# One encoder layer on one core: the values of two head groups by seven block products, the reversed rows gathered in steps, the kept weights prepared earlier

## The chip, the cores and the metric

The kernel runs on one core of a Trainium2 chip. The metric is the device time of one execution in microseconds (us). The engines are TensorE (PE in the profile, its weight loads PEld), VectorE (DVE), ScalarE (ACT), GpSimd (POOL) and SyncE (SP). SP and GpSimd also issue the DMA transfers. Each engine takes its instructions in the order in which the program lists them and waits at an instruction whose data aren't there.

## The reference, cut to what matters

One layer of an encoder, sequence 1024, width 1024, all in float32:

```
h = LN1(alpha*x + 0.5*SwiGLU_a(x))
h = LN2(alpha*h + HybridMixer(h))
h = LN3(alpha*h + 0.5*SwiGLU_b(h))

SwiGLU(x) = (silu(x @ w_gate) * (x @ w_up)) @ w_down        # inner width 2752
HybridMixer: p = h @ w_in + b_in  ->  q | k | v | u | gates
  attention: 12 heads in 3 groups of 4 with (window, dilation) = (128,1), (512,4), (2048,16)
  fourier:   real part of an FFT over positions and channels of u
  out = (g_attn * (attn @ w_proj_attn) + g_four * (four @ w_proj_fourier)) @ w_out
```

The change concerns v: `v = h @ w_in[:, v columns] + b_in[v columns]`, a product of 1024 x 1024 with 1024 x 1536. Its columns fall into three head groups of 512.

## The kernel before, in words

**Products.** Every float32 operand of a big product is split into a high and a low part (`split`, L324: ScalarE writes the high part at L330, VectorE the low one at L334), and each product runs as three matmuls: high by high, high by low, low by high (`TERMS`). One matmul is 128 x 128 by 128 x 512. The products of the feed-forward blocks and of the paired columns of the mixer (u, q with k, gates) are done in 2 x 2 blocks by seven block products in place of eight (`PROD`, L346: Winograd's form of Strassen's method). With rows in two halves and the inner dimension in two halves, the row operand has blocks a11, a12, a21, a22 and the sums s1 to s4 (`Operand.derive`, L385 and after), the weights have b11 to b22 and the sums t1 to t4. A pair of column blocks c takes seven jobs `J[c, 1..7]` of 12 matmuls.

**Order of the work.** The order is not written out by hand. Each piece is a node of a planner (`Flow`, L73): PE jobs in a fixed list, tasks for VectorE (V) and ScalarE (S, which stands for GpSimd's issues as well), loads (Q), and floating PE work (F). A node has a cost, what it depends on, a due job (`need`), a lead, and what it takes and gives back of three pools: 8 PSUM banks, `NPG` = 46 pages (128 x 1024) and `NS2` = 11 half pages. The planner steps through the jobs on a clock of its own and writes the program in the order that comes out. A load is put in the program when the due time less the lead is reached; a load that is far from due leaves 6 pages free. On the chip only the data's own waits hold; the planner's clock sets the order alone.

**The stages.** Feed-forward a: pairs of gate and up columns (a0 to a20) and a tail, its hidden blocks spilled to DRAM (`hsa...`), the weight sums for the down product made in DRAM (`tdat`: SP copies one block, L701, GpSimd adds another by an accumulating DMA, L704). Then the down product of block a (L741): block products 1, 6, 2, 5, 3, 7, 4, each in 11 steps of 12 matmuls, each step's operands loaded (L729, L730) with a lead of 44 us and split. Then norm 1 and its transposes (`tpY`), which give the row operand X2 (tiles `Ya...`) of the mixer. Then the values, the pairs u0, u1, q0 to q11 (with attention beside them) and s0 to s7, the two projections, the output product, norm 2, and feed-forward block b.

**The values before** (L1015 to L1051). Three groups of 512 columns, each 8 row tiles of 128 by one job of 24 matmuls: 8 inner blocks by three terms, into one bank. The order is group 0 rows 0 to 511, group 1 rows 0 to 511, group 0 rows 512 to 1023, group 1 rows 512 to 1023, group 2. Each group's weights are 4 pages, loaded by SP (L1029) and split. VectorE adds the bias (L1049) and GpSimd spills the result to `v_spill` (L1050), from which attention loads it later. `X2.derive` makes the blocks for the values and the sums s1 to s4 for the first u pair.

**The gather** (`reversed_rows`, L995). When pair a10's first product is done, GpSimd issues one after the other: the load of an index, an indirect load of 128 rows of `w_proj_fourier`, its store to `w_rev`, the second indirect load, its store. The two pages it takes are given back together.

**The kept weights** (`keep_parts`, L1400 and after). The two projections' weights (`wpa`, `wpf`, four quarters each) are loaded, the Fourier ones folded with the reversed rows (L1447, L1448), split, and the parts stored to DRAM (L1418), to be loaded again when the projections run. All eight are due at the job `early`, which is the first product of pair u0, with leads of 60 us (load) and 52 us (split).

Of the kernel before, what the change touches and what calls it, by code (L numbers as in the profile page):

```python
# [13 lines left out]
OP = mybir.AluOpType  # L14
AX = mybir.AxisListType

P = 128
S0 = 1024
D = 1024
KD = 8  # L20
# [52 lines left out]
class Flow:  # L73
# [21 lines left out]
    def V(self, *a, **kw):  # L95
        return self.task("V", *a, **kw)

    def S(self, *a, **kw):
        return self.task("S", *a, **kw)

    def Q(self, need, mb, fn, deps=(), lead=24.0, **kw):
        self.loads.append(Node("Q", mb, fn, deps, need, lead, **kw))
        return self.loads[-1]

    def F(self, us, fn, deps=(), banks=0, **kw):
        self.floats.append(Node("F", us, fn, deps, banks=banks, **kw))
        return self.floats[-1]
# [152 lines left out]
class Builder:  # L260
# [16 lines left out]
    def bank(self, name):  # L277
        return self.pp.tile([P, 512], F32, name=name, tag="ps", bufs=8)
# [6 lines left out]
def kernel(  # L285
# [38 lines left out]
    def split(name, get, put, deps=(), need=None, lead=14.0, w=1024, pages=2, gives=1):  # L324

        st = {}

        def hi():
            st["h"] = page(name + "h", F32R)
            nc.scalar.activation(st["h"][:, :w], get()[:, :w], AF.Copy)  # L330

        def lo():
            t = page(name + "l", F32R)
            nc.vector.tensor_sub(t[:, :w], get()[:, :w], st["h"][:, :w].bitcast(F32))  # L334
# [11 lines left out]
    PROD = {1: ("a11", "b11"), 2: ("a12", "b21"), 3: ("s4", "b22"), 4: ("a22", "t4"),  # L346
            5: ("s1", "t1"), 6: ("s2", "t2"), 7: ("s3", "t3")}
# [573 lines left out]
    X1, X2, X3 = Operand("X"), Operand("Y"), Operand("Z")  # L921
# [24 lines left out]
    COL_Q, COL_K, COL_V = 0, QW, 2 * QW  # L946
# [7 lines left out]
    w_rev = kb.dram([2 * P, D], "w_rev")  # L954
# [38 lines left out]
        return [S(0.0, lambda h=h: shears(h), [(n, 6.0 + 3.0 * h)]) for h in range(NH)]  # L993

    def reversed_rows():  # L995
        st = {}

        def gather():
            idx = kb.small([P, 2], "rev_idx", mybir.dt.int32)
            nc.gpsimd.dma_start(idx, c_rev)  # L1000
            for t in range(2):
                pg = page(f"rev{t}")
                nc.gpsimd.indirect_dma_start(out=pg, out_offset=None, in_=w_pf,
                                             in_offset=bass.IndirectOffsetOnAxis(ap=idx[:, t:t + 1], axis=0))
                nc.gpsimd.dma_start(w_rev[t * P:(t + 1) * P, :], pg)
        n = S(0.0, gather, [J[("a", 10), 1]], slack=20.0, pages=2)
        fl.later(n, 12.0, gives=2)
        return n

    shear_n = mixer_consts()  # L1010
# [1 line left out]


    v_d = kb.dram([S0, QW], "v_spill")
    VJ, v_stored = {}, {}  # L1015
# [3 lines left out]
    VJ[2, 7].back["p"] += 4  # L1019
    VW, vb = {}, {}  # L1020
    for g in range(3):
        def bias_row(g=g):
            vb[g] = half(f"vb{g}")
            nc.gpsimd.dma_start(vb[g], bcast_rows(b_in[COL_V + g * 512:COL_V + (g + 1) * 512], 512))
        qb = Q(VJ[g, 0], 0.25, bias_row, halves=1)
        for i in range(4):
            def load(i=i, g=g):
                VW[g, i] = t = page(f"wv{g}{i}")
                nc.sync.dma_start(t, in_values[g, i])  # L1029
            split(f"wv{g}{i}", lambda g=g, i=i: VW[g, i], lambda t, g=g, i=i: VW.__setitem__((g, i), t),  # L1030
                  [Q(VJ[g, 0], 0.5, load, pages=1)], VJ[g, 0], 20.0 if g else 14.0)
        VJ[g, 7].back["p"] += 8
        for m in range(8):
            st = {}

            def run(g=g, m=m, st=st):
                hf, mm = divmod(m, 4)
                ms = slice(mm * P, (mm + 1) * P)
                st["b"] = ps = bank(f"v{g}{m}")
                for k in range(KD):  # L1040
                    wv = [t.rearrange("p (k n) -> p k n", k=2)[:, k % 2, :] for t in VW[g, k // 2]]
                    for ti, (a, b) in enumerate(TERMS):
                        nc.tensor.matmul(ps, X2.cols(f"a{hf + 1}{k // 4 + 1}", a, k % 4)[:, ms], pick(wv, b),  # L1043
                                         start=(k == 0 and ti == 0), stop=(k == KD - 1 and ti == 2))
            VJ[g, m].fn = run

            def store(g=g, m=m, st=st):
                t = half(f"vs{g}{m}")
                nc.vector.tensor_add(t, st["b"], vb[g])  # L1049
                nc.gpsimd.dma_start(v_d[m * P:(m + 1) * P, g * 512:(g + 1) * 512], t)  # L1050
            v_stored[g, m] = V(0.69, store, [VJ[g, m], qb], frees=1, halves=1)  # L1051
            fl.later(v_stored[g, m], 3.0, hgives=1 + (m == 7))


    HEADS = [(g, h) for h in range(SLOTS) for g in range(3)]
# [7 lines left out]
    for g in range(3):  # L1063
        for m in range(8):
            VJ[g, m].after(*[X2.node[f"a{m // 4 + 1}{kh + 1}", i] for kh in range(2) for i in range(2)])
    for c in pairs:
        pair_weights(PC[c], in_pairs)
        for p in PROD:
# [470 lines left out]
    for gi in range(4):  # L1539
        st = {}  # L1540
# [6 lines left out]
        for i in range(2):  # L1547
# [24 lines left out]
            f = F(0.88, run, [q, (chan_ready, 10.0)], 1, gives=i)  # L1572
            n = S(0.42, hi, [f], pages=1 if s_ == 0 else 0, slack=2.0)
# [41 lines left out]
    for t in range(2):  # L1615
        st = {}
# [51 lines left out]
    f = F(1.7, mid_run, fold_n[0, 0] + fold_n[1, 0] + [pos_parts["n", 0]], 2)  # L1668
# [17 lines left out]
    n = V(0.6, mid_raw, [PJ[2]], pages=2, slack=20.0)  # L1686
# [12 lines left out]
    for c in range(8):  # L1699
        c2, cc = divmod(c, 2)  # L1700
        st = {}
# [20 lines left out]
    for c in range(8):  # L1722
        c2, cc = divmod(c, 2)
        st = {}
# [59 lines left out]
    for m in range(8):  # L1784
        st, sums = {}, kb.small([P, 4], "lw", bufs=9)
# [137 lines left out]
```

## Time and profile before

| | |
|---|---|
| median of three runs | 2103.39 us (2102.98 to 2103.85) |
| the profiled execution | 2102.25 us |
| its span, first to last instruction | 2100.5 us |
| mean granted TensorE clock | 0.998 |
| PE busy, weight loads busy | 2081.6 us (99%), 1732.6 us (82%) |
| VectorE, ScalarE, GpSimd busy | 1353.3, 766.6, 234.9 us |
| value matmuls (L1043) | 6.2% of the chain that ended last |

The profile is of one execution. Its page gives busy time by engine, the span in 40 slices, DMA queues, the chain of work that ended last, the costliest groups of instructions with what they waited for, and the DMA issues with their time to landing. The trace behind it can be asked for the instructions in order of time, for waits, and for busy time by stretches. In a row of a timeline the first number is the start in us from the span's start, the second the duration, and the bracket at the end the idle time of the engine before it and what ended that.

### The profile page before, as it was taken

Reading aid. Unit: us, or ns where it says so; the run is one execution under the profiler, and the core shown is the slowest. Engines: PE = TensorE matmul, PEld = TensorE weight load, DVE = VectorE, ACT = ScalarE, POOL = GpSimd, SP = SyncE. Lnnn points to the kernel's source line nnn. Section 1 sums busy time; section 2 is a strip of 40 time slices with the busy share of each in tenths; the row PEclk is TensorE's granted clock in tenths of the full one; section 3 lists DMA queues with packets and bytes.
Section 4 is the critical chain, followed back from the end, with each engine's and each line's share of the span. In section 5 each row is a group of like instructions: output and inputs, shape, how many; then the busy total and the mean of one; then the engine's idle time right before and its main releaser. Section 6 shows DMA issues by size and latency. Waiting matters only on the chain.

```text
span 2100.5 us, 25488 instructions
## 1 busy us (share of the span) xinstructions
PE 2081.6 (99%) x9619; PEld 1732.6 (82%) x9619; DVE 1353.3 (64%) x1856; ACT 766.6 (36%) x1175; POOL 234.9 (11%) x411
## 2 busy tenths in 40 slices
PE   9999999999999999999999999999999999999998
PEld 7888888888888888888888888888788888888886
DVE  6766666673575278556666654767766666675566
ACT  4322222362353132444445433315332222245332
POOL 0121211000001120022132101000001001010000
PEclk9999999999999999999999999999999999999999
DMA  4357876596643275567876439432223223267753
GB/s 160 126 181 218 256 191 192 162 342 224 207 174 142 84 277 147 173 166 201 216 200 168 167 126 370 156 136 101 86 91 116 95 90 136 82 232 273 235 180 105
DMA packets 141658, 366.66 MB, mean 175 GB/s; under 512 B 18066, under 2 KB 40338, under 8 KB 141152
## 3 DMA queue, kind: packets, MB, share of 16 engines
q1 hardware_dynamic: 104608, 244.36, 33.6%
q0 software_dynamic: 36928, 120.68, 19.7%
q8 instruction: 75, 1.23, 0.2%
q14 instruction: 47, 0.39, 0.1%
HBM read 277.18 MB, written 137.06 MB: 197 GB/s over the span
## 4 chain that ended last, share of the span: by engine, by line
PE 86%; issue 2%; DVE 1%; ACT 0%; DMA 0%; POOL 0%; DVEq 0%; POOLq 0%; ACTq 0%
PE Bb L422 7%; PE v L1043 6%; PE Ab L422 5%; PE Db L422 5%; PE Bq L422 5%; PE Ba L422 4%; PE Dq L422 3%; PE Aq L422 3%; PE Bs L422 3%; PE Zb L741 3%; PE Xb L741 3%; PE Za L741 3%; PE Xa L741 3%; PE Da L422 2%; PE wo L1798 2%; PE Aa L422 2%
## 5 line engine op out<-in xcount | busy, mean ns | idle before, releaser
L1049 DVE TENSOR_TENSOR vs<-v,vb 128x512 f32<-128x512 f32 x24 | 16.5, 691 | 61.0 <-PE v L1043 60.7
L1293 ACT ACTIVATE p<-p,stat 128x192 f32<-128x192 f32 (+2 forms) x96 | 42.3, 442 | 24.6 <-DVE stat L1288 23.9
L533 POOL DMA_DIRECT2D hsba<-r2b x19 | 10.3, 543 | 329.8 <-DVE r2b L603 329.8
L1280 DVE SCALAR_TENSOR_TENSOR p<-sc,bias 128x512 f32<-128x512 f32 (+1 forms) x40 | 24.8, 620 | 27.9 <-PE sc L1266 21.6
L533 POOL DMA_DIRECT2D hsaa<-r2a x19 | 11.0, 580 | 282.0 <-DVE r2a L603 282.0
L1325 PEld LDWEIGHTS pv<-pT,v 128*128 128x128 f32 (+1 forms) x320 | 37.1, 189 | 5.2
L1325 PE MATMUL pv<-pT,v 128*128 128x128 f32 (+1 forms) x320 | 40.6, 289 | 0.0
L501 ACT ACTIVATE r1a<-Aa 128x512 f32<-128x512 f32 x19 | 11.3, 597 | 73.0 <-PE Aa L422 73.0
L509 DVE TENSOR_TENSOR r3q<-Bq,r1q 128x512 f32<-128x512 f32 x12 | 8.3, 691 | 42.8 <-PE Bq L422 42.8
L587 ACT ACTIVATE sga<-Aa 128x512 f32<-128x512 f32 x19 | 11.4, 599 | 64.7 <-PE Aa L422 64.7
L587 ACT ACTIVATE sgb<-Ab 128x512 f32<-128x512 f32 x19 | 11.4, 598 | 63.8 <-PE Ab L422 63.8
L509 DVE TENSOR_TENSOR r3b<-Bb,r1b 128x512 f32<-128x512 f32 x19 | 13.1, 692 | 32.7 <-PE Bb L422 32.7
L590 DVE TENSOR_TENSOR r3b<-Db,r3b 128x512 f32<-128x512 f32 x19 | 13.1, 691 | 32.5 <-PE Db L422 32.5
L1266 PE MATMUL sc<-oq,oq 128*128 128x192 f32 (+2 forms) x192 | 33.8, 322 | 0.0
L590 DVE TENSOR_TENSOR r3a<-Da,r3a 128x512 f32<-128x512 f32 x19 | 13.1, 691 | 29.3 <-PE Da L422 29.1
L1266 PEld LDWEIGHTS sc<-oq,oq 128*128 128x128 f32 x192 | 29.9, 190 | 2.0
L1467 POOL DMA_DIRECT2D comb_t<-stat x48 | 29.2, 616 | 10.9 <-DMA stat<-stat 10.9
L501 ACT ACTIVATE r1b<-Ab 128x512 f32<-128x512 f32 x19 | 11.4, 598 | 47.7 <-PE Ab L422 47.7
L939 POOL DMA_DIRECT2D y_spill<-y x8 | 4.3, 537 | 215.3 <-DVE y L907 215.3
L493 DVE TENSOR_TENSOR usa<-ua,usa 128x512 fp32r<-128x512 f32 x19 | 13.1, 692 | 21.0 <-ACT usa L489 20.9
L422 PE MATMUL Da<-Xs40h,usa 128*128 128x512 f32 x76 | 26.5, 389 | 0.0
L422 PE MATMUL Da<-Xs41h,usa 128*128 128x512 f32 x76 | 26.5, 389 | 0.0
(7408 smaller groups left out, 7252.8 us busy)
## 6 DMA issues: line engine op xcount, KB each, us to landing
qa<-hsas SPq DMA_DIRECT2D x44, 256.0 KB, 3.8
qa<-tdat SPq DMA_DIRECT2D x44, 256.0 KB, 4.2
qb<-hsbs SPq DMA_DIRECT2D x44, 256.0 KB, 4.4
ga<-in_ffn_gu_dram SPq DMA_DIRECT2D x21, 512.0 KB, 4.2
ua<-in_ffn_gu_dram SPq DMA_DIRECT2D x21, 512.0 KB, 6.2
gb<-in_ffn_gu_dram SPq DMA_DIRECT2D x21, 512.0 KB, 3.5
ub<-in_ffn_gu_dram SPq DMA_DIRECT2D x21, 512.0 KB, 3.7
qa<-hsaa SPq DMA_DIRECT2D x33, 256.0 KB, 5.3
```

Of the source, the lines that this page charges most:

```text
L422: nc.tensor.matmul(out, pick(w, a)[:, k * P:(k + 1) * P], self.cols(xn, b, k), start=first and k == 0 and ti == 0, stop=last and k == 3 an ...
L501: nc.scalar.activation(H[c, "t1"], B[c, "A"], AF.Copy)
L587: nc.scalar.activation(H[c, "s0"], B.pop((c, "A")), AF.Silu)
L590: nc.vector.tensor_sub(H[c, "t3"], B[c, "D"], H[c, "t3"])
L741: nc.tensor.matmul(B[tag, set_, m], pick(q, a)[:, m * P:(m + 1) * P], pick(q, b)[:, R], start=first and j == 0 and ti == 0, stop=j == PAIR ...
L1043: nc.tensor.matmul(ps, X2.cols(f"a{hf + 1}{k // 4 + 1}", a, k % 4)[:, ms], pick(wv, b), start=(k == 0 and ti == 0), stop=(k == KD - 1 and ...
L1266: nc.tensor.matmul(sv[:, i, :], qk[0][:, qt * P:(qt + 1) * P], qk[1][:, k0:k0 + w], start=True, stop=True, skip_group_check=True)
L1280: stt(p3(), sv, scale, bv, op0=OP.mult, op1=OP.add)
L1293: nc.scalar.activation(p3()[:, i, :], p3()[:, i, :], AF.Exp, bias=stats[h][:, k, 0:1], scale=1.0, accum_out=stats[h][:, k, 1:2])
L1325: nc.tensor.matmul(out_of(tiles.index(qt)), env["v"][kc, rows], pt[r0:r0 + rows, sl * P:(sl + 1) * P], start=qt not in seen, stop=last, sk ...
L1467: nc.gpsimd.dma_start(dst, bass.AP(tensor=sd.tensor, offset=sd.offset + 48 * p0 + 2 * col, ap=ap))
L1798: nc.tensor.matmul(bk[i], pick(merged[k], a)[:, ms], pick(wo[k], b)[:, i * 512:(i + 1) * 512], start=(k == 4 * gi and ti == 0), stop=(k == ...
```

## The change: what it does

Three things, in one diff.

**Values of groups 0 and 1.** These two groups now form the two column blocks of one 2 x 2 block product: rows in two halves, inner dimension in two halves, columns group 0 and group 1. Seven block products (`VORDER`) replace eight; each is four jobs (one for each of four row tiles) of 12 matmuls into the banks A (products 1, 2), B (6, 7, 4) and D (5, 3). Group 2 keeps its jobs, now called `VJ["g", m]`: its rows 0 to 511 come first, then products 1 and 2, then its rows 512 to 1023, then products 6, 7, 5, 4, 3. The weights' sums t1 to t4 are made in DRAM ahead of time, as the down product's are: an SP copy due at the first product of pairs a2 to a5 and an accumulating GpSimd DMA due at the fifth product of pairs a3 to a6, 1 MB each. VectorE makes the result blocks from the banks (`value_sums`) with bias rows of its own. `X2.derive` is due at the value products in place of the first u pair.

**The gather** is issued in steps: the index when pair a6's first product is done, then gather, store, gather, store, each 16 us (on the planner's clock) after the one before, one page at a time, given back 6 us after its store.

**The kept weights** are due at step 8 of product 2 of the first down product (`J["a", "d", 2, 8]`).

```diff
-        def gather():
-            idx = kb.small([P, 2], "rev_idx", mybir.dt.int32)
-            nc.gpsimd.dma_start(idx, c_rev)
-            for t in range(2):
-                pg = page(f"rev{t}")
-                nc.gpsimd.indirect_dma_start(out=pg, ...
-                nc.gpsimd.dma_start(w_rev[t * P:(t + 1) * P, :], pg)
-        n = S(0.0, gather, [J[("a", 10), 1]], slack=20.0, pages=2)
-        fl.later(n, 12.0, gives=2)
+        st, n = {}, S(0.0, lambda: nc.gpsimd.dma_start(idx, c_rev), [J[("a", 6), 1]], slack=20.0)
+        for t in range(2):
...
+            n = S(0.0, gather, [(n, 16.0)], slack=20.0, pages=1)
+            n = S(0.0, store, [(n, 16.0)], slack=20.0)
+            fl.later(n, 6.0, gives=1)
...
-    for g, hf in ((0, 0), (1, 0), (0, 1), (1, 1), (2, 0), (2, 1)):
-        for m in range(4 * hf, 4 * hf + 4):
-            VJ[g, m] = job(24 * MM, None, 1)
+    VORDER = ((1, "A", True), (2, "A", False), (6, "B", True), (7, "B", False), (5, "D", True), (4, "B", False),
+              (3, "D", False))
+    def value_job(p, bk, new):
+        def product(m):
...
+                xn, wn = PROD[p]
+                for k in range(4):
+                    w = [t.rearrange("p (k n) -> p k n", k=2)[:, k % 2, :] for t in VW[wn, k // 2]]
+                    for ti, (a, b) in enumerate(TERMS):
+                        nc.tensor.matmul(B["v", bk, m], X2.cols(xn, a, k)[:, m * P:(m + 1) * P], pick(w, b), ...
+        for m in range(4):
+            VJ[p, m] = job(12 * MM, product(m), int(new), gives=4 if m == 3 else 0)
+    for m in range(4):
+        VJ["g", m] = job(24 * MM, None, 1)
+    for p, bk, new in VORDER:
+        value_job(p, bk, new)
+        if p == 2:
+            for m in range(4, 8):
+                VJ["g", m] = job(24 * MM, None, 1)
+    VJ["g", 7].back["p"] += 12
+    for i, (to, x0, x1) in enumerate((("t1", "b11", "b12"), ("t3", "b12", "b22"), ("t2", "t1", "b22"),
+                                      ("t4", "t2", "b21"))):
+        def copy(to=to, x0=x0):
+            nc.sync.dma_start(vt[to], vblk[x0] if x0 in vblk else vt[x0])
+        def add(to=to, x1=x1):
+            nc.gpsimd.dma_start(vt[to], vblk[x1], accum_op=OP.add, max_dma_last_dim=4096)
+        n = Q(J[("a", 2 + i), 1], 1.0, copy, [vtn[x0]] if x0 in vtn else [], lead=0.0)
+        vtn[to] = Q(J[("a", 3 + i), 5], 1.0, add, [n], lead=0.0)
...
+        n1 = V(0.69, t1, [VJ[1, m], q1], VJ[2, m], pages=new_page)
+        v_stored[0, m] = V(0.69, c11, [VJ[2, m], n1], frees=1, halves=1)
+        n2 = V(0.69, t2, [n1, VJ[6, m]], VJ[7, m], halves=1)
+        n3 = V(0.69, t3, [n2, VJ[7, m]], VJ[4, m], pages=new_page)
+        n4 = v_stored[1, m + 4] = V(0.69, c22, [n3, VJ[5, m]], VJ[3, m], halves=1, gives=m % 2)
+        n5 = V(0.4, z21, [n3, qs])
+        v_stored[0, m + 4] = V(0.69, c21, [n5, VJ[4, m]], frees=1, halves=1, gives=m % 2)
+        v_stored[1, m] = V(0.69, c12, [n4, VJ[3, m]], frees=1)
...
-    X2.derive({"a11": VJ[0, 0], "a12": VJ[0, 0], "a21": VJ[0, 4], "a22": VJ[0, 4]},
-              {p: J[PC["u", 0], p] for p in PROD}, 30.0)
+    X2.derive({"a11": VJ["g", 0], "a12": VJ["g", 0], "a21": VJ["g", 4], "a22": VJ["g", 4]},
+              {p: VJ[p, 0] for p in PROD}, 30.0)
...
-    early = J[PC["u", 0], 1]
+    early = J["a", "d", 2, 8]
```

More of the change, by code (lines that the diff above doesn't have):

```diff
@@ L995, in reversed_rows, with gather, store @@
     def reversed_rows():
-        st = {}
-        def gather():
-            idx = kb.small([P, 2], "rev_idx", mybir.dt.int32)
-            nc.gpsimd.dma_start(idx, c_rev)
-            for t in range(2):
-                pg = page(f"rev{t}")
-                nc.gpsimd.indirect_dma_start(out=pg, out_offset=None, in_=w_pf,
-                                             in_offset=bass.IndirectOffsetOnAxis(ap=idx[:, t:t + 1], axis=0))
-                nc.gpsimd.dma_start(w_rev[t * P:(t + 1) * P, :], pg)
-        n = S(0.0, gather, [J[("a", 10), 1]], slack=20.0, pages=2)
-        fl.later(n, 12.0, gives=2)
+        idx = kb.small([P, 2], "rev_idx", mybir.dt.int32)
+        st, n = {}, S(0.0, lambda: nc.gpsimd.dma_start(idx, c_rev), [J[("a", 6), 1]], slack=20.0)
+        for t in range(2):
+            def gather(t=t):
+                st[t] = page(f"rev{t}")
+                nc.gpsimd.indirect_dma_start(out=st[t], out_offset=None, in_=w_pf,
+                                             in_offset=bass.IndirectOffsetOnAxis(ap=idx[:, t:t + 1], axis=0))
+            def store(t=t):
+                nc.gpsimd.dma_start(w_rev[t * P:(t + 1) * P, :], st[t])
+            n = S(0.0, gather, [(n, 16.0)], slack=20.0, pages=1)
+            n = S(0.0, store, [(n, 16.0)], slack=20.0)
+            fl.later(n, 6.0, gives=1)
         return n
@@ L1014 @@
     v_d = kb.dram([S0, QW], "v_spill")
-    VJ, v_stored = {}, {}
-    for g, hf in ((0, 0), (1, 0), (0, 1), (1, 1), (2, 0), (2, 1)):
-        for m in range(4 * hf, 4 * hf + 4):
-            VJ[g, m] = job(24 * MM, None, 1)
[L1019 to L1041, printed above, removed]
-                    for ti, (a, b) in enumerate(TERMS):
[L1043 to L1052, printed above, removed]
@@ new lines, with run @@
+    VJ, v_stored, VW, vb, VT = {}, {}, {}, {}, {}
+    VORDER = ((1, "A", True), (2, "A", False), (6, "B", True), (7, "B", False), (5, "D", True), (4, "B", False),
+              (3, "D", False))
+    def value_job(p, bk, new):
+        def product(m):
+            def run():
+                if new:
+                    B["v", bk, m] = bank(f"v{bk}{m}")
+                xn, wn = PROD[p]
+                for k in range(4):
+                    w = [t.rearrange("p (k n) -> p k n", k=2)[:, k % 2, :] for t in VW[wn, k // 2]]
+                    for ti, (a, b) in enumerate(TERMS):
+                        nc.tensor.matmul(B["v", bk, m], X2.cols(xn, a, k)[:, m * P:(m + 1) * P], pick(w, b),
+                                         start=new and k == 0 and ti == 0, stop=k == 3 and ti == 2,
+                                         skip_group_check=True)
+            return run
+        for m in range(4):
+            VJ[p, m] = job(12 * MM, product(m), int(new), gives=4 if m == 3 else 0)
@@ new lines, in value_row, with run, value_part, load @@
+    def value_row(key, g, need):
+        def run():
+            vb[key] = half(f"vb{key}")
+            nc.gpsimd.dma_start(vb[key], bcast_rows(b_in[COL_V + g * 512:COL_V + (g + 1) * 512], 512))
+        return Q(need, 0.25, run, halves=1)
+    def value_part(name, i, src, deps, need, lead):
+        def load():
+            VW[name, i] = t = page(f"wv{name}{i}")
+            nc.sync.dma_start(t, src)
+        split(f"wv{name}{i}", lambda: VW[name, i], lambda t: VW.__setitem__((name, i), t),
+              [Q(need, 0.5, load, deps, lead + 10.0, pages=1)], need, lead)
@@ new lines, in store_values, with run, store @@
+    def store_values(t, m, g):
+        nc.gpsimd.dma_start(v_d[m * P:(m + 1) * P, g * 512:(g + 1) * 512], t)
+    q2 = value_row(2, 2, VJ["g", 0])
+    for i in range(4):
+        value_part("g2", i, in_values[2, i], (), VJ["g", 0], 14.0)
+    for p, bk, new in VORDER:
+        n = PROD[p][1]
+        for i in range(2):
+            value_part(n, i, (vblk if n in vblk else vt)[n][i], [vtn[n]] if n in vtn else (), VJ[p, 0], 14.0)
+    for m in range(8):
+        st = {}
+        def run(m=m, st=st):
+            hf, mm = divmod(m, 4)
+            st["b"] = ps = bank(f"v{m}")
+            for k in range(KD):
+                wv = [t.rearrange("p (k n) -> p k n", k=2)[:, k % 2, :] for t in VW["g2", k // 2]]
+                for ti, (a, b) in enumerate(TERMS):
+                    nc.tensor.matmul(ps, X2.cols(f"a{hf + 1}{k // 4 + 1}", a, k % 4)[:, mm * P:(mm + 1) * P], pick(wv, b),
+                                     start=(k == 0 and ti == 0), stop=(k == KD - 1 and ti == 2))
+        VJ["g", m].fn = run
+        def store(m=m, st=st):
+            t = half(f"vs{m}")
+            nc.vector.tensor_add(t, st["b"], vb[2])
+            store_values(t, m, 2)
+        v_stored[2, m] = V(0.69, store, [VJ["g", m], q2], frees=1, halves=1)
+        fl.later(v_stored[2, m], 3.0, hgives=1 + (m == 7))
@@ new lines, with both_rows, value_sums, page_half @@
+    q0, q1 = value_row(0, 0, VJ[1, 0]), value_row(1, 1, VJ[1, 0])
+    def both_rows():
+        vb["s"] = half("vbs")
+        nc.vector.tensor_add(vb["s"], vb[0], vb[1])
+    qs = V(0.4, both_rows, [q0, q1], VJ[6, 0], halves=1)
+    def value_sums(m):
+        def page_half(key):
+            k, i = (key, m // 2), m % 2
+            if k not in VT:
+                VT[k] = page(f"v{key}{m // 2}")
+            return VT[k][:, i * 512:(i + 1) * 512]
+        def t1():
+            nc.vector.tensor_sub(page_half("t1"), B["v", "A", m], vb[1])
+        def c11():
+            t = half(f"v00{m}")
+            nc.vector.tensor_add(t, B.pop(("v", "A", m)), vb[0])
+            store_values(t, m, 0)
+        def t2():
+            VT["t2", m] = t = half(f"vt2{m}")
+            nc.vector.tensor_add(t, B["v", "B", m], VT["t1", m // 2][:, (m % 2) * 512:(m % 2) * 512 + 512])
+        def t3():
+            nc.vector.tensor_add(page_half("t3"), B["v", "B", m], page_half("t1"))
+        def c22():
+            t = half(f"v11{m}")
+            nc.vector.tensor_sub(t, B["v", "D", m], page_half("t3"))
+            store_values(t, m + 4, 1)
+        def z21():
+            nc.vector.tensor_add(page_half("t1"), page_half("t1"), vb["s"])
+        def c21():
+            t = half(f"v01{m}")
+            nc.vector.tensor_add(t, B.pop(("v", "B", m)), page_half("t1"))
+            store_values(t, m + 4, 0)
+        def c12():
+            t = VT.pop(("t2", m))
+            nc.vector.tensor_sub(t, B.pop(("v", "D", m)), t)
+            store_values(t, m, 1)
+        new_page = 1 if m % 2 == 0 else 0
+        n1 = V(0.69, t1, [VJ[1, m], q1], VJ[2, m], pages=new_page)
[6 more added lines that the diff above has]
+        v_stored[1, m] = V(0.69, c12, [n4, VJ[3, m]], frees=1)
+        for key in ((0, m), (1, m + 4), (0, m + 4), (1, m)):
+            fl.later(v_stored[key], 3.0, hgives=1)
@@ L1055 @@
+    for m in range(4):
+        value_sums(m)
+    S(0.0, lambda: None, [v_stored[0, m] for m in range(4)] + [qs], hgives=2)
+    S(0.0, lambda: None, [v_stored[0, m] for m in range(4, 8)], hgives=1)
     HEADS = [(g, h) for h in range(SLOTS) for g in range(3)]
```

10 lines of the change are left out of this document (7 added, 3 removed).

## The prediction

> **What bounds the kernel now.** I read the page's head, then the chain that ended last through the stage that changes, then busy time by stretches.
>
> ```profile
> span 2100.5 us, 25488 instructions
> PE 2081.6 (99%) x9619; PEld 1732.6 (82%) x9619; DVE 1353.3 (64%) x1856; ACT 766.6 (36%) x1175; POOL 234.9 (11%) x411
> PE 86%; issue 2%; DVE 1%; ACT 0%; DMA 0%; POOL 0%; DVEq 0%; POOLq 0%; ACTq 0%
> ```
>
> ```profile
> 644.34 5.44 PE v L1043 x24
> 649.78 0.93 PE tpY L373 x8
> 650.71 5.51 PE v L1043 x24
> 656.22 2.62 PE tpY L373 x24
> 658.84 119.72 PE v L1043 x528
> 778.56 2.72 PE Au L422 x12
> ```
>
> TensorE (PE) is busy through the span and the chain is PE. Busy time alone could flatter it, since matmuls overlap; the second fence settles it. The value product (L1043) runs as 576 matmuls, 528 of them in one unbroken piece of 119.72 us, which is 0.2267 us each; 24 take 5.44 us, the same pace; and the next product (Au) starts where the last value matmul ends. So here a matmul fewer is 0.2267 us less, as long as nothing else ends last.
>
> The other engines and the DMA, by stretches (columns: length, busy us of PE, PEld, VectorE, ScalarE, GpSimd with counts, granted clock, DMA share, GB/s):
>
> ```profile
> 440.00:460.00 20.00, 20.00 (x90) 16.56 (x89) 17.49 (x16) 13.81 (x13) 0.00 (x0) 1.00 1.04 387
> 460.00:520.00 60.00, 60.00 (x266) 49.69 (x265) 22.83 (x25) 21.66 (x23) 0.00 (x0) 1.00 0.72 245
> 520.00:580.00 60.00, 60.00 (x266) 49.69 (x265) 35.05 (x41) 22.10 (x21) 0.00 (x0) 1.00 0.60 193
> 680.00:720.00 40.00, 40.00 (x178) 33.12 (x177) 6.08 (x9) 4.25 (x4) 4.58 (x9) 1.00 0.15 53
> 720.00:780.00 60.00, 60.00 (x267) 49.69 (x266) 43.52 (x49) 15.97 (x16) 14.64 (x28) 1.00 0.76 276
> ```
>
> The first three lie in the first down product, which ends at 644, the last two in the value stage. PE is full and its clock whole in all. VectorE idles in 680 to 720, and DMA has room almost everywhere; 387 GB/s is the most that a row here shows.
>
> **Part 1: the values of two groups by seven block products.** Removed: 16 products of 24 matmuls, 384. Added: 7 block products x 4 row tiles x 12 matmuls, 336, of the same shape and pace. Group 2 keeps its 192. So 48 matmuls go: 48 x 0.2267 = **-10.88 us** on PE, if the new order never makes it wait. What could make it wait:
>
> ```profile
> L1049 DVE TENSOR_TENSOR vs<-v,vb 128x512 f32<-128x512 f32 x24 | 16.5, 691 | 61.0 <-PE v L1043 60.7
> 668.37 1.22 DVE L334 TENSOR_TENSOR Ya221l<-Ya,Ya221h 128x1024 fp32r<-128x1024 f32 x1
> 709.01 1.06 ACT L330 ACTIVATE wv20h<-wv 128x1024 fp32r<-128x1024 f32 x1 [45.12 <-PE v L1043]
> 760.85 0.68 DVE L1447 TENSOR_TENSOR wpf3s<-wpf 128x512 f32<-128x512 f32 x1
> wv<-in_in_values_dram SPq DMA_DIRECT2D x12, 512.0 KB, 5.1
> ```
>
> VectorE: 24 additions of 0.691 us become 8 for group 2, 32 for the block sums and one of bias rows, 17 more, +11.7 us; weight splits go from 12 to 18, 6 x 1.22 = +7.3 us; the four kept-weight preparations that leave (part 3) take away 8 x 1.22 + 8 x 0.68 = 15.2 us. Net +3.8 us, in a stage whose two rows above hold 49.6 of 100 us: covered on average. The operand's s1 to s4 are now wanted by product 6, not by the u pair. The last row split they wait for ends at 669.6 (668.37 + 1.22). Product 6 stands after 8 products of group 2 and 8 block products: 644.34 + 3.55 of transposes + 12 x 5.44 = 713.2. That leaves 43.6 us for six sums and the first two splits, 8 x 1.22 = 9.8 us. Within the block products each PSUM sum has 3 jobs of 2.72 us between the product it reads and the next one on that bank, against 0.69. Costed at nothing; if that cover went, one sum is 0.69 us.
>
> Pages are the tight resource. NPG is 46; row 709.01 shows the price of waiting for them: ScalarE stood 45.12 us until a value product released pages. After the change the four a21 pages and the eight of group 2 come back only when g7 ends, just as product 6 begins. By my count from the code about 44 are then held (32 of the row operand and its sums, 8 of group 2, 4 of weights or value sums, 2 of LN constants, less what was given back). Product 7's two weight pages may start loading only then: landing 5.1, ScalarE 1.06, VectorE 2 x 1.22, in sum 8.6 us against the 10.88 us of product 6: covered, by 2.3 us. If product 6's own weights had to wait so, nothing would cover it: 8.6 us. Bounds 0 and +8.6; a gain is excluded, since PE already runs there without a gap. I take **+0.7**, near the covered end, since only a late DMA or a busy VectorE uses up the 2.3 us.
>
> **Part 2: the weight sums in DRAM.** Four copies on SP's queue and four accumulating stores on GpSimd's, 1 MB each, beside the first pairs of the first feed-forward block. The DMA has room: 162 GB/s in 100 to 140 below. The chain is what matters: the copy for t4 waits on SP until the add for t2 has landed, and the weight loads of pair a7 stand behind it.
>
> ```profile
> 100.00:140.00 40.00, 40.00 (x176) 32.31 (x175) 28.21 (x43) 10.73 (x14) 9.80 (x20) 1.00 0.48 162
> 113.65 0.33 SPq L452 DMA_DIRECT2D ga<-in_ffn_gu_dram  x1
> 118.24 0.33 SPq L452 DMA_DIRECT2D ua<-in_ffn_gu_dram  x1
> 122.82 0.51 POOL L982 DMA_DIRECT2D lines_d<-line  x1 [0.33 <-DVE line L981]
> 137.62 1.05 ACT L330 ACTIVATE ga7h<-ga 128x1024 fp32r<-128x1024 f32 x1
> 147.48 0.69 DVE L590 TENSOR_TENSOR r3a<-Da,r3a 128x512 f32<-128x512 f32 x1 [2.03 <-PE Da L422]
> tdat<-in_ffn_down_dram POOLq DMA_DIRECT2D x8, 1024.0 KB, 11.7
> ga<-in_ffn_gu_dram SPq DMA_DIRECT2D x21, 512.0 KB, 4.2
> ```
>
> The add for t2 stands on GpSimd behind the three lines_d stores, by its due time (fifth product of pair a5), so it goes at about 123.4 and lands 11.7 us later, at 135.1. The add for t4 in turn holds GpSimd until its copy lands; behind it stand spills of the hidden blocks, which nobody reads before the down product: no cost. Only then can SP go on; a7's load, until now at 113.65, lands at 139.3, 1.7 us after ScalarE's split ga7h took place at 137.62. ScalarE and VectorE work in order, so what stands behind that split moves with it, up to r3a, which PE needs; row 147.48 shows 2.03 us of idle VectorE there as cover. Bounds 0 and +4 (both loads and a whole split on PE's path); I take **+0.5**. The Trainium skill (DMA: Bandwidth & Descriptors, section Anatomy of one DMA) fits a GpSimd DMA as 2.0 us plus the bytes at 436 GB/s, an estimate of 4.4 us for 1 MB; the trace's 11.7 us for an accumulating one disagrees, and by the page this term would be zero and the time 2092.8.
>
> **Part 3: the gather in steps.** Now GpSimd issues index, gather, store, gather, store in one go and waits inside:
>
> ```profile
> 220.06 1.92 POOL L1003 DMA_INDIRECT rev<-in_w_proj_fourier_dram,rev_idx  x1 [4.13 <-ACT t12a11h L330]
> 234.09 0.56 POOL L1005 DMA_DIRECT2D w_rev<-rev  x1 [6.70 <-DMA rev<-in_w_proj_fourier_dram,rev_idx]
> 237.28 1.22 DVE L334 TENSOR_TENSOR ga12l<-ga,ga12h 128x1024 fp32r<-128x1024 f32 x1 [2.07 <-DMA w_rev<-rev]
> 242.25 0.39 PE L422 MATMUL Da<-Xs11h,t12a11l 128*128 128x512 f32 x1
> 242.90 0.50 PE L422 MATMUL Ba<-Xa220h,t34a11h 128*128 128x512 f32 x1 [0.26 <-DVE r3a L509]
> ```
>
> The second store is issued at 234.09; the split that gets its page waits 2.07 us, and PE starts two matmuls 0.65 us apart instead of 0.23: 0.42 us lost. With 16 us between gather and store, and between store and next gather, that wait goes; next late there is nothing but PE. **-0.42** (0 to -0.65).
>
> **Part 4: the kept weights beside the down product.** Their due time moves from product Au at 778.56 to step 8 of down product 2, three steps of 2.72 us before product 5 begins:
>
> ```profile
> 460.82 0.32 SPq L729 DMA_DIRECT2D qa<-hsas  x1
> 520.63 59.84 PE Za L741 x264
> ```
>
> That is 512.5, and with a lead of 60 us the first load comes at about 452. So 8 loads and 16 stores of 0.52 MB, 12.6 MB, and VectorE's 15.2 us move into 452 to 520. VectorE has 22.83 of 60 us there, and GpSimd, whose queue takes the stores, has nothing at all. DMA: 387 - 245 = 142 GB/s free gives 8.5 MB in the 60 us; the other 4.1 MB run on into 520 to 580, which has room for 11.6. On SP the eight loads stand among the loads of the down steps. Their cover is prefetch: the step loaded at 460.82 is multiplied from 520.63 on, 59.8 us later. Costed at **0**; without that cover it is the second rival. The gathers come four pairs earlier and are done long before 452. In the value stage the same work leaves the stretch 720 to 780, so its load falls.
>
> **The sum.** -10.88 + 0.7 + 0.5 - 0.42 + 0 = -10.10 us. The profiled execution took 2102.25 us (span 2100.5), so 2092.15 there; the median of the runs shown, 2103.39, stands 1.14 above it. Forecast: **2093.3 us**. A measurement of this kernel tells about 0.2% from no change, 4.2 us: faster means below 2099.2, slower above 2107.6.
>
> **Rival one, no change: pages at product 6.** If product 6's own weights, or the pages for s2, come free only when g7 ends, the 8.6 us stand whole on PE's path, in place of the 0.7: 2093.3 - 0.7 + 8.6 = 2101.2. For it: the count of about 44 of 46 pages, and ScalarE's 45.12 us wait for pages in this very stage. Against: before, two groups' weights (16 pages) were held at once beside the operand and PE ran 528 matmuls without a gap.
>
> **Rival two, slower: the down product runs dry.** The kept weights take pages and DMA time from the prefetch of the steps. If the prefetch is used up, PE waits for the 4.1 MB that don't fit, 4.1 / 387 GB/s = 10.6 us, and at worst also for the 15.2 us of VectorE work put ahead of its own splits: 10.6 to 25.8, middle 18. That gives 2111. It decides from a wait of 14.3 us on. For it: row 440 to 460, where DMA is at 387 GB/s and VectorE at 17.49 of 20. Against: the 59.8 us of prefetch and the light rows after it. The Trainium skill (HBM Reference, Specifications) gives a core about 358 GB/s as its share; the row of 387 lies above that, and by the page 5.8 MB would be left over, 16.2 us for the 10.6.
>
> **Rival three, a smaller gain: late loads in the first pairs.** If the waits of part 2 cost their bound, 4 us for 0.5, the time is 2096.8. For it: the 0.42 us that PE lost to one such wait. Against: 2.03 us of cover and one chain only.
>
> That the change doesn't do what it says I leave out: the matmuls are counted in the diff, and their pace stands in the trace.
>
> **How the numbers follow.** Forecast 0.78, rival one 0.09, rival two 0.07, rival three 0.06. Faster: 0.78 + 0.06 = 0.84; same 0.09; slower 0.07. The low end is -10.88 - 0.65 without any new wait, 2091.9, less half the spread of the runs shown (2102.98 to 2103.85): 2091.4. The high end takes in rival three and half of part 1's bound beside it (2096.8 - 0.7 + 4.3, shortened to the edge of faster): 2099.0. Left out are rivals one and two, 0.16.
>
> **What would show it.** In the changed kernel the value matmuls should come to 528, in pieces that together with the transposes last 123 to 124 us from the end of the down product to Au; a gap at product 6 or 7, with a ScalarE split ended by PE or a DMA, means part 1's pages. In the first pairs an SP row that waits for an accumulating store, and a ScalarE split of ga7 that waits for its DMA, means part 2; PE's two starts near 243 should be 0.23 us apart. In 452 to 580 PE should stay at 60 of 60 us, with DMA share near 1. I am wrong if PE shows gaps there, or if the value stage saves 10.9 us and the span doesn't.

## The result, and the profile after

| | kernel before | changed kernel |
|---|---|---|
| median of six runs | 2103.24 us (2102.69 to 2103.85) | 2091.45 us (2091.06 to 2092.26) |
| ratio, 95% interval | | 0.9945 (0.9935 to 0.9955) |
| profiled execution, its span | 2102.25, 2100.5 us | 2091.71, 2089.9 us |

The change saves 11.79 us by the medians and 10.5 us by the profiled executions; the one of before was quicker than every run in the table, and this accounts for most of the difference. The forecast was 2093.3 in a range of 2091.4 to 2099.0, and the result stands near its quick end.

The head of the changed kernel's page and its chain that ended last:

```profile
span 2089.9 us, 25459 instructions
PE 2071.5 (99%) x9571; PEld 1724.3 (83%) x9571; DVE 1371.5 (66%) x1879; ACT 773.3 (37%) x1181; POOL 237.3 (11%) x415
PE 97%; issue 1%; DVE 1%; ACT 0%; DMA 0%; SPq 0%; DVEq 0%
```

PE has 48 matmuls fewer (9619 to 9571) and 10.1 us less of busy time; the span is 10.6 us shorter. The chain through the value stage (start, length, what) shows where:

```profile
645.26 5.44 PE v L1090 x24
...
659.75 10.89 PE v L1090 x48
670.64 21.76 PE vA L1029 x96
692.40 21.76 PE v L1090 x96
714.16 21.76 PE vB L1029 x96
735.92 10.88 PE vD L1029 x48
746.80 10.88 PE vB L1029 x48
757.68 10.88 PE vD L1029 x48
768.56 2.72 PE Au L422 x12
```

From 659.75 on each piece begins where the one before it ends, product 6 at 714.16 included. The stage takes 768.56 - 645.26 = 123.30 us; before it took 778.56 - 644.34 = 134.22. That is 10.92 us, against 10.88 by the count. The other stretches, the first of them at the program's start (columns as in the prediction):

```profile
10.00:20.00 10.00, 10.00 (x35) 7.98 (x34) 6.07 (x6) 7.53 (x9) 0.00 (x0) 0.76 1.14 462
460.00:520.00 60.00, 60.00 (x266) 49.71 (x265) 39.75 (x39) 29.49 (x32) 8.45 (x16) 1.00 1.05 391
520.00:580.00 60.00, 60.00 (x266) 49.67 (x266) 36.50 (x41) 27.04 (x26) 0.00 (x0) 1.00 0.78 276
720.00:780.00 60.00, 60.00 (x267) 49.67 (x266) 40.83 (x50) 14.21 (x15) 6.49 (x12) 1.00 0.32 114
```

The kept weights are now in 460 to 520: VectorE up from 22.83 to 39.75 us, GpSimd from nothing to 16 stores, 391 GB/s, and PE without a gap. The value stage's DMA share falls from 0.76 to 0.32. The weight sums' chain in the first pairs, from the timelines of GpSimd, SP and ScalarE, and behind them one line of the chain that ended last:

```profile
124.58 1.00 POOL L1054 DMA_DIRECT2D vtt<-in_in_values_dram  x1
132.75 0.48 SPq L1051 DMA_DIRECT2D vtt<-vtt  x1
133.32 0.53 SPq L452 DMA_DIRECT2D ga<-in_ffn_gu_dram  x1
141.98 1.06 ACT L330 ACTIVATE ga7h<-ga 128x1024 fp32r<-128x1024 f32 x1 [2.95 <-DMA ga<-in_ffn_gu_dram]
```

```profile
148.69 2.96 PE Ba L422 x12
```

The add for t2 goes at 124.58; SP stands at t4's copy until 132.75, and only then issues a7's load; ScalarE waits 2.95 us for it. Of that PE sees next to nothing: the product behind r3a takes 2.96 us for its 12 matmuls instead of 2.72. VectorE's idle time covers the rest: the 2.03 us that it had ahead of r3a (row 147.48 of the prediction) are used up.

### The profile page after: what moved, and what is told of

Same layout as the page of the kernel before. It is cut to its first block, busy times and chain, and to the rows that moved or that the text cites. A ratio compares the mean times of both kernels' runs of the same rounds, so it can differ in the third digit from the quotient of the medians.

```text
span 2089.9 us, 25459 instructions
## 1 busy us (share of the span) xinstructions
PE 2071.5 (99%) x9571; PEld 1724.3 (83%) x9571; DVE 1371.5 (66%) x1879; ACT 773.3 (37%) x1181; POOL 237.3 (11%) x415
## 4 chain that ended last, share of the span: by engine, by line
PE 97%; issue 1%; DVE 1%; ACT 0%; DMA 0%; SPq 0%; DVEq 0%
PE Bb L422 7%; PE Ba L422 7%; PE Aa L422 5%; PE Ab L422 5%; PE Db L422 5%; PE Da L422 5%; PE Bq L422 5%; PE Dq L422 3%; PE Aq L422 3%; PE Bs L422 3%; PE Zb L741 3%; PE Xb L741 3%; PE Za L741 3%; PE Xa L741 3%; PE wo L1910 3%; PE pj L1823 2%
## 5 line engine op out<-in xcount | busy, mean ns | idle before, releaser
L509 DVE TENSOR_TENSOR r3b<-Bb,r1b 128x512 f32<-128x512 f32 x19 | 13.1, 691 | 32.7 <-PE Bb L422 32.7
L590 DVE TENSOR_TENSOR r3b<-Db,r3b 128x512 f32<-128x512 f32 x19 | 13.1, 691 | 32.5 <-PE Db L422 32.5
L590 DVE TENSOR_TENSOR r3a<-Da,r3a 128x512 f32<-128x512 f32 x19 | 13.1, 691 | 28.9 <-PE Da L422 28.8
L493 DVE TENSOR_TENSOR usa<-ua,usa 128x512 fp32r<-128x512 f32 x19 | 13.1, 692 | 21.0 <-ACT usa L489 20.9
L422 PE MATMUL Db<-Zs40h,usb 128*128 128x512 f32 x76 | 26.5, 389 | 0.0
L422 PE MATMUL Db<-Zs41h,usb 128*128 128x512 f32 x76 | 26.5, 389 | 0.0
```

The costliest lines, as they stand in the source:

```text
L422: nc.tensor.matmul(out, pick(w, a)[:, k * P:(k + 1) * P], self.cols(xn, b, k), start=first and k == 0 and ti == 0, stop=last and k == 3 an ...
L590: nc.vector.tensor_sub(H[c, "t3"], B[c, "D"], H[c, "t3"])
```

## The experiments

**Which part earns the time.** Three parts can be put in or left out by themselves. The parts are the values with their weight sums, the gather, and the place of the kept weights.

`seven_only`: the seven products with their sums in DRAM.

```diff
 # changed kernel, with the old reversed_rows and
-    early = J["a", "d", 2, 8]
+    early = J[PC["u", 0], 1]
```

> The seven block products with their sums in DRAM alone; gather and kept weights as before. Theory (the number of matmuls sets the time, all else is covered): 48 x 0.2267 = 10.9 us less than before, 2092.3, with the 0.42 us gap near 243 still there. Rival (the parts lean on each other): the kept weights, back in the value stage, take 15.2 us of VectorE and pages from products 6 to 3, and PE waits there by 3 to 9 us: 2095 to 2101, with gaps between the value pieces.

Measured: 2112.41 us (2111.86 to 2113.03), ratio 1.0044 (1.0027 to 1.0061). The part that takes 48 matmuls away makes the kernel slower when it stands alone, and the theory of its expectation falls. PE's waits (us in total, times, longest):

```profile
PE Ba L422 <- DVE r3a L509: 7.2, 1, 7.2
PE vD L1028 <- ACT wvb220h L330: 3.6, 1, 3.6
PE vD L1028 <- DVE wvt10l L334: 1.4, 1, 1.4
```

There are two main places: one in the pairs near 250 us, behind the old gather, and one at the last value products, at the splits of their weights. The rival of the expectation, that the parts lean on each other, had the second place but not the first.

`gather_only` and `early_only` put one of the other parts alone into the kernel before; `no_seven` puts in both.

```diff
 # gather_only: kernel before, with the new reversed_rows
 # early_only: kernel before, with
-    early = J[PC["u", 0], 1]
+    early = J["a", "d", 2, 8]
 # no_seven: kernel before, with both
```

> The gather in steps alone. Theory: the gap near 243 goes, 0.4 us less, 2102.8, within what a measurement tells; seen in the trace by PE starts 0.23 us apart there. Rival (the gather brings what the change gained beyond 10.9 us): 0.9 us or more less.

> The kept weights due beside the down product, alone. Theory: no change, 2103.2, PE at 60 of 60 us in 460 to 520 and in 520 to 580, DMA share there near 1. Rival (the down product pays for it and the value stage gains it back): PE gaps in 452 to 600 and a time over 2104.

> Gather in steps and early kept weights, with the values in eight block products as before. Theory: 2102.8, 11 us and more above the changed kernel: all of the gain is the seven products'. Rival (the other two parts bring a share of it): under 2101.

Measured: 2102.2 us, ratio 0.9995 (0.9985 to 1.0004); 2103.72, 1.0002 (0.9993 to 1.0012); 2102.37, 0.9996 (0.9987 to 1.0006). None can be told from no change. The gather's 0.42 us is too small to be confirmed by time.

So the parts do not add up one by one, and the two losses of `seven_only` were separated next.

**`seven_early`**: the changed kernel with the old gather.

```diff
-    (reversed_rows in timed steps, begun at pair a6)
+    (reversed_rows of the kernel before: index, gather, store, gather, store at pair a10)
```

> The changed kernel with the gather of before (one step at a10, the store directly behind it); the seven products and the kept weights beside the down product stay. Theory A (two separate losses): this one keeps the gather's loss alone, 2091.5 + 7.4 + about 5 for the half clock = 2101 to 2105 us, one PE gap of 6 to 8 us near 250 us with the clock at half behind it, and a value stage of 123 to 124 us. Theory B (the kept weights' place is the cause, and the gather's gap in the first of the two was chance): 2091.5 + 0.4 = about 2092 us, gap near 243 to 250 us under 1 us.

Measured: 2101.21 us, ratio 0.9993 (0.9984 to 1.0003), so 9.76 us above the changed kernel. From the timelines of GpSimd and VectorE, then the chain, the stretches and PE's wait:

```profile
238.13 0.55 POOL L1005 DMA_DIRECT2D w_rev<-rev  x1 [9.66 <-DMA rev<-in_w_proj_fourier_dram,rev_idx]
245.03 1.23 DVE L334 TENSOR_TENSOR ga12l<-ga,ga12h 128x1024 fp32r<-128x1024 f32 x1 [8.78 <-DMA w_rev<-rev]
```

```profile
238.13 6.71 DMA w_rev<-rev
...
250.64 5.49 PE Ba L422 x12
256.13 2.98 PE Da L422 x12
```

```profile
240.00:250.00 10.00, 3.68 (x17) 2.71 (x15) 3.75 (x5) 1.06 (x1) 1.18 (x2) 0.81 0.99 214
250.00:260.00 10.00, 9.36 (x29) 7.46 (x30) 5.73 (x9) 1.69 (x2) 0.00 (x0) 0.68 0.48 103
```

```profile
PE Ba L422 <- DVE r3a L509: 7.0, 1, 7.0
PE Ba L422 <- DVE t12a20l L334: 0.8, 1, 0.8
```

The split ga12l has no use for the reversed rows, yet it waits for their second store: its page was the gather's, and the rows must have left it. Before, GpSimd waited 6.70 us for the second gather and the split 2.07; here it is 9.66 and 8.78, and PE stands 7.0 us. Then the clock is granted in part only (0.81 and 0.68), and the 24 matmuls that follow take 5.49 + 2.98 in place of 5.44 us: 3.0 us more. 7.0 + 3.0 = 10.0. The second wait, near 416 us, puts PE another 1.1 us behind; it stands in `seven_only` too, but neither in the changed kernel nor in the kernel before, and where it comes from stays open. The profiled execution took 10.85 us more than that of the changed kernel, the median of ten 9.76. Counting gives nearly the same for the first place: 17 + 29 matmuls in 20 us, where 88 fit, are 42 x 0.2267 = 9.5 us lost.

**`gather_a10`**: the changed kernel with its gather begun four pairs later, where the old one stood.

```diff
-        st, n = {}, S(0.0, lambda: nc.gpsimd.dma_start(idx, c_rev), [J[("a", 6), 1]], slack=20.0)
+        st, n = {}, S(0.0, lambda: nc.gpsimd.dma_start(idx, c_rev), [J[("a", 10), 1]], slack=20.0)
```

> The changed kernel with its gather in timed steps, but begun at pair 10 as in the kernel before instead of at pair 6; all else as changed. The 7.0 us gap of the kernel with the old gather ends a chain of ga12l waiting for the second store of reversed rows (6.71 us), because that split's page was a page of the gather. Theory T: what costs is a page that is given back by a time in the plan before its store has landed, and the steps of 16 us cure that wherever the gather begins; then no PE gap over 0.5 us follows between 220 and 300 us, and the time is 2091 to 2093 us. Theory L: what costs is the place, the loads of pair 11 and 12 beside the gather; then a gap of 3 to 8 us stands between 230 and 300 us with half clock behind it, and the time is 2095 to 2104 us.

Measured: 2090.91 us (2090.61 to 2091.31), ratio 0.9943 (0.9926 to 0.9959), no more than the changed kernel. GpSimd and VectorE, and one stretch, at the place where `seven_early` stood still:

```profile
236.61 0.57 POOL L1005 DMA_DIRECT2D w_rev<-rev  x1 [3.14 <-DMA rev<-in_w_proj_fourier_dram,rev_idx]
236.22 1.22 DVE L334 TENSOR_TENSOR ga12l<-ga,ga12h 128x1024 fp32r<-128x1024 f32 x1
```

```profile
220.00:260.00 40.00, 40.00 (x178) 33.15 (x177) 26.13 (x35) 11.49 (x15) 9.47 (x12) 1.00 0.78 224
```

GpSimd waits for a gather here too, and the DMA is no quieter (its share in 220 to 240 is 1.04, for 0.79 in `seven_early`), but ga12l runs at 236.22 without a wait, ahead even of the store's issue: the page it gets isn't that of a gather under way. So not the place of the gather was wrong but the early return of its pages, 12 us on the planner's clock after a step that on the chip took 24 us, from the first gather at 220.90 to the landing of the second store at 244.84. Theory T holds; theory L, that the loads of those pairs were the cause by themselves, falls. The steps change the spacing of the transfers as well as the pages' return, and no run parts the two; it is the wait for a store that the split doesn't read that points to the pages. Why the second gather itself lands later with the seven products (9.66 for 6.70 us) stays open: beside it SP issues the loads of a12 and a13 (224.44 to 234.71), of which before only those of a12 stood there (216.87 and 223.44) and a13's came at 237.01, behind it. (The expectation calls them pairs 11 and 12.)

**`no_early`**: the changed kernel with the kept weights left beside the value products.

```diff
-    early = J["a", "d", 2, 8]
+    early = J[PC["u", 0], 1]
```

> The changed kernel with the kept weights left where they were, beside the value products; the seven products and the gather in two steps stay. Theory A, from the kernel with the seven products alone: two separate losses made it slower, 7.4 us and a half clock of 10.2 us (some 5 us more) behind the old gather, and about 7 us with 6.8 us at half clock in the value products, where the kept weights' loads and stores share the queues with the products' own weights. By it this kernel keeps the second loss alone: 2091.5 + 6 to 10 = 2097 to 2102 us, no PE gap near 250 us, PE waits of 1 to 4 us for wv... splits near 774 us, and a value stage of 130 to 134 us. Theory B: the old gather is the one cause and disturbs the rest of the run; then this kernel takes 2091 to 2093 us, with the stage at 123 to 124.

Measured: 2101.19 us, ratio 0.9996 (0.9986 to 1.0005), 9.74 us above the changed kernel. Of this kernel the timelines of SP and ScalarE, then the chain, a stretch, and PE's wait:

```profile
747.31 0.38 SPq L1548 DMA_DIRECT2D wpa<-in_w_proj_attn_dram  x1
752.14 2.57 SPq L1067 DMA_DIRECT2D wvb<-in_in_values_dram  x2
757.90 1.06 ACT L330 ACTIVATE wpa3eh<-wpa 128x1024 fp32r<-128x1024 f32 x1 [9.56 <-DMA wpa<-in_w_proj_attn_dram]
761.90 1.06 ACT L330 ACTIVATE wvb220h<-wvb 128x1024 fp32r<-128x1024 f32 x1 [0.24 <-DMA wvb<-in_in_values_dram]
```

```profile
740.91 5.84 DMA wpf_d<-wpf0eh
...
749.23 1.37 SPq L1552
```

```profile
720.00:780.00 60.00, 53.52 (x221) 42.73 (x220) 48.59 (x58) 20.30 (x20) 14.96 (x28) 0.94 0.83 300
```

```profile
PE vD L1029 <- ACT wvb220h L330: 4.1, 1, 4.1
```

The same row of the changed kernel's SP:

```profile
728.21 8.07 SPq L1067 DMA_DIRECT2D wvb<-in_in_values_dram  x2
```

Product 3's weights (wvb) are loaded behind the last quarter of the kept weights, 24 us later than in the changed kernel, and that quarter's load comes late itself: the chain runs from the store of a kept part (wpf_d, landed at 746.75) through the splits that wait for its page to SP's load (L1552). ScalarE's split of wvb stands behind the splits of that quarter and then waits another 0.24 us for its own load. PE waits 1.4 us for a split of product 5's weights as well and 0.8 us for the low part of wvb. It has 221 matmuls in the 60 us in place of 267: 46 x 0.2267 = 10.4 us. Both runs came as theory A had them: two separate losses, each with its own part. So both parts that are worth nothing alone are worth 9.7 to 9.8 us each beside the seven products (the kernel before, run beside each of them, had medians from 2102.5 to 2103.4):

| values | gather | kept weights | us |
|---|---|---|---|
| before | before | before | 2103.24 |
| before | steps | before | 2102.2 |
| before | before | early | 2103.72 |
| before | steps | early | 2102.37 |
| seven | before | before | 2112.41 |
| seven | steps | before | 2101.19 |
| seven | before | early | 2101.21 |
| seven | steps | early | 2091.45 |

From 2112.41, 9.74 and 9.76 make 19.5 of the 21.0 us.

**The pages** (`pages44`, `pages42`): the changed kernel with a smaller pool.

```diff
-NPG = 46
+NPG = 44
```

(42 in the second kernel.)

> The changed kernel with 44 pages in place of 46. Theory of the forecast (about 44 pages are held when group 2's last product ends, and product 7's weights have 2.3 us to spare): PE waits a few us at product 6 or 7, 2093 to 2100. Rival (the stage has pages to spare, so its count was too high): value pieces without a gap, within 1 us of the changed kernel.

> The changed kernel with 42 pages. Theory of the forecast: product 6's own weights wait for group 2's pages, 8.6 us and more in the value stage, and other stages lose too: over 2101. Rival: still no gap in the value stage, whatever other stages lose.

Measured: 2105.48 us (2103.5 to 2107.71), ratio 1.0012 (1.0002 to 1.0022), and 2130.23, 1.0131 (1.0111 to 1.0151). PE's waits in the value stage, of the first and then of the second:

```profile
PE vB L1029 <- DVE wvt21l L334: 1.5, 1, 1.5
```

```profile
PE vB L1029 <- DVE wvt20l L334: 1.7, 1, 1.7
PE vB L1029 <- DVE wvt21l L334: 1.7, 1, 1.7
```

wvt2 is the weight of product 6, the place that rival one of the prediction named. So pages do run short there, from 44 down, but PE waits for them 1.5 and 3.4 us at this product; the rest of the 14 and 39 us is spread over the whole kernel.

**The down product's cover** (`store_twice`, `store_half`): every store of a kept part made twice, or every other one.

```diff
+        spare = [kb.dram([P, 1024], f"{name}_x{i}") for i in range(2)]
...
                 nc.gpsimd.dma_start(dst[i], st["p"][i].bitcast(F32))
+                nc.gpsimd.dma_start(spare[i], st["p"][i].bitcast(F32))
```

(With `if i == 0:` ahead of the new store in `store_half`.)

> The changed kernel, with each part of the kept weights stored a second time to a spare place in DRAM: 8.4 MB more in 452 to 580, pages held longer. Theory (prefetch covers the DMA's backlog): PE stays at full in the down product, within 1 us of the changed kernel; the step loads run behind by up to 8.4 MB / 390 GB/s = 21.5 us more. Rival (the prefetch is nearly used up): PE waits in 480 to 600, 3 to 21 us longer.

> The changed kernel with every other store of a kept part made twice (half the extra bytes of the run that stored all twice, which had its loads of x rows 20.3 us later and a PE wait of 13.1 us). If the cover is what those two numbers leave, about 7 us, half the extra bytes make the loads some 10 us late, PE waits 3 us (2 to 5) for the addition into ya, 3.4 us at half clock follow, and the time is 2091.5 + 3 to 7 = 2094 to 2098 us. Rival: the wait does not grow in step with the bytes, because VectorE's order and not the bytes sets it; then it is 0 (time 2091 to 2092) or still 10 us and more (over 2100).

Measured: 2106.37 us (2104.44 to 2107.3), ratio 1.0015 (1.0004 to 1.0025), and 2095.45 (2094.62 to 2096.07), 0.9966 (0.9953 to 0.9978). The loads of x rows (first and last start), PE's wait and the stretch 520 to 580, first of `store_twice`, then of `store_half`; for the changed kernel stands the row of its loads alone:

```profile
L942 SPq DMA_DIRECT2D ya<-in_x_dram x8: 328/328/333, 528.9 to 544.2; - x8
PE Za L741 <- DVE ya L831: 13.1, 1, 13.1
520.00:580.00 60.00, 46.89 (x197) 38.35 (x196) 39.70 (x44) 29.59 (x28) 0.00 (x0) 0.89 0.98 368
```

```profile
L942 SPq DMA_DIRECT2D ya<-in_x_dram x8: 327/328/333, 516.9 to 532.1; - x8
PE Za L741 <- DVE ya L831: 2.0, 1, 2.0
520.00:580.00 60.00, 57.97 (x249) 47.59 (x248) 39.42 (x43) 29.58 (x29) 0.00 (x0) 0.97 0.91 331
```

```profile
L942 SPq DMA_DIRECT2D ya<-in_x_dram x8: 327/330/372, 508.6 to 523.9; - x8
```

The last loads are 20.3 and 8.2 us later than in the changed kernel, and PE waits 13.1 and 2.0 us: in both some 6 to 7 us of the delay are covered, and the rest falls on PE whole, through VectorE, whose addition into ya stands behind splits that wait for late loads. In matmuls: 266 - 197 = 69 and 266 - 249 = 17, 15.6 and 3.9 us; measured 14.9 and 4.0. The rival that the wait has nothing to do with the bytes falls. So the second rival's mechanism is real, and the changed kernel stands some 7 us short of it.

**The weight sums' chain** (`chain_free`): t4's copy and add two pairs later, so that SP's copy meets an add that has landed.

```diff
-        n = Q(J[("a", 2 + i), 1], 1.0, copy, ...
-        vtn[to] = Q(J[("a", 3 + i), 5], 1.0, add, [n], lead=0.0)
+        n = Q(J[("a", 2 + i + 2 * (i == 3)), 1], 1.0, copy, ...
+        vtn[to] = Q(J[("a", 3 + i + 2 * (i == 3)), 5], 1.0, add, [n], lead=0.0)
```

> The changed kernel, with the copy for t4 due two pairs later (and its add too), so that SP need not wait for the add of t2. Theory: the loads of pair a7 are issued near 114 again, ScalarE's split ga7h no longer waits 2.95 us for its DMA, and PE gets back 0.1 to 0.2 us near 148.7, too little to measure. Rival (the wait costs the 0.5 us of the forecast or more): 0.5 us less and over.

Measured: 2091.13 us (2090.25 to 2091.38), ratio 0.9944 (0.9927 to 0.996). ScalarE's split comes 3.2 us earlier and waits for nothing:

```profile
138.78 1.05 ACT L330 ACTIVATE ga7h<-ga 128x1024 fp32r<-128x1024 f32 x1
```

The chain is there as the prediction described it, and taking it away gains 0.3 us at most, which these runs cannot tell from none. In the traces PE's matmuls behind r3a come 0.2 us earlier. `chain_free` and `gather_a10` are the two quickest of all kernels run, by less than the spread of the runs.

## Why the prediction was right, point by point

- **The 48 matmuls, -10.88:** the stage shows -10.92. Right.
- **Waits for pages, +0.7:** none came. With two pages less, 1.5 us came, at product 6 and not at product 7, which the prediction had down as the tight one. So pages are near their end there as it said, but the whole load of 8.6 us, its upper bound, did not come even with four pages less.
- **The weight sums' chain, +0.5:** the chain ran as told (add at 124.58 for 123.4 predicted, ScalarE's split late), but SP was free 8.2 us after the add was issued, not 11.7, and VectorE's idle time covered nearly all. Matmul by matmul PE falls 0.22 us further behind the kernel before at this place: mis-sized by some 0.3 us. The estimate of 4.4 us for such a transfer by the Trainium skill (DMA: Bandwidth & Descriptors, section Anatomy of one DMA) remains too short beside the 8.2 us here. Another 0.32 us, which the prediction doesn't have, go at pair a2 (65 us), where PE waits 1.2 us for r2a in place of 0.9; it is so in every kernel of 46 pages with the seven products and in none without them, and what delays r2a stays open.
- **The gather, -0.42:** the wait is gone from the profile; PE's two starts are 0.23 us apart. At the first it is 1.49 us behind the kernel before (243.74 for 242.25), at the second 1.07 (243.97 for 242.90): 0.42 us made up, as forecast, and 0.1 us more just behind it. By time it couldn't be confirmed.

```profile
243.74 0.39 PE L422 MATMUL Da<-Xs11h,t12a11l 128*128 128x512 f32 x1
243.97 0.39 PE L422 MATMUL Ba<-Xa220h,t34a11h 128*128 128x512 f32 x1
```

- **The kept weights, 0:** PE had no gap in 460 to 580. Right in the changed kernel, but the cover named was the wrong one: the prediction counted 59.8 us of prefetch, and the row of 485.76 below shows step loads 35.8 us ahead of their use; what the runs with more bytes leave is 6 to 7 us, set by the addition into ya.

```profile
485.76 0.32 SPq L729 DMA_DIRECT2D qa<-hsas  x1
...
521.57 59.84 PE Za L741 x264
```

- **The sum:** -10.10 forecast against the profiled execution, -10.54 found there. By stretches: up to the value stage +0.92 (its begin at 645.26 for 644.34) where +0.08 was forecast, in the stage -10.92 for -10.18, behind it -0.54 for 0, of which 0.4 lie behind the last matmul. The first is the program's start, +0.92 by 17 us, and then the three places above, +0.32, +0.22 and -0.5, which all but cancel. At the start PE waits 2.9 us for its first weight split in place of 2.5, and the clock granted in 10 to 20 us is 0.76 in place of 0.87. This belongs to the execution and not to the change: `store_half`, which starts as the changed kernel does, has 2.4 us and 0.83 there, and `gather_only`, which starts as the kernel before does, has 3.2 us and 0.77 and is as late. So it is in part luck that the sum came so near: the slow start takes back the 0.7 us for pages that were not lost. The medians differ by more, 11.79, since the one of before lies 0.99 above its profiled execution and the one of after 0.26 below.
- **What the sum didn't see:** it added four parts as if each had its own price. With the seven products alone the kernel would have been 9 us slower, and two parts priced at -0.42 and 0 are what makes the gain appear: they take away a late page and a late load that the seven products' new order would otherwise have met. The number came out right because all three parts were there, not because each had been priced for its own effect. The prediction looked for the slower case in the down product; it lay nearer in the value stage and behind the old gather. It said that the load of the value stage would fall by part 4, but drew no price from it.

## What to carry to other kernels

Price the parts of a change together: ask of each part what it would meet if the others weren't there, for a step that saves nothing alone can be the one that lets another step's saving reach the end. A page given back on a planner's clock is free only when its last DMA has landed; look in the trace for a split whose wait is for a transfer that it doesn't use. And a stretch's loss is quickly read by counting PE's instructions in it against an undisturbed one: that count includes the slow clock behind a gap, which a list of waits leaves out.

## What the runs showed of the hardware

A PE gap costs more than its length. Behind the 7.0 us gap of `seven_early` the granted clock was 0.81 and 0.68 in two stretches of 10 us, and 24 matmuls took 3.0 us more, the first 12 of them 5.49 us for 2.72; behind the 13.1 us of `store_twice` the 60 us from 520 had 0.89 and a total loss of 15.6 us. The Trainium skill (TensorE: Matmul & The Clock Gate, section Part 1: The HAM clock gate) says that an idle window of about 3.4 us halves the clock until a busy one has passed; the runs agree for the long gaps; the 2.0 us of `store_half`, shorter than that, stand with 0.97 in their stretch, and 3.9 us were lost there, so a shorter gap can cost more than itself too.

The DMA moved 391 GB/s over 60 us of the changed kernel, and 462 GB/s in the stretch from 10 to 20 us, beyond the 387 that the prediction took as its ceiling; the kernel before had moved 414 in that first stretch already. The 358 GB/s from the Trainium skill (HBM Reference, Specifications) that the prediction set against it is a share with both cores of a pair at work; the same section puts a core alone well above it, and the row agrees.
